# Attention readout with the values as the stationary operand, in two column halves, and denominators from the exponentials' running sums

## The chip, the cores and the metric

The program runs on one core of one Trainium2 chip. Times are device microseconds (us) of one execution; the figure that counts is the median of several. Engine names: PE is TensorE (PEld is its weight load), DVE is VectorE, ACT is ScalarE, POOL is GpSimd, SP is the engine that issues the weight DMAs.

## The reference, cut to what matters

Two layers over 256 tokens of width 1024. Layer 0 is a gated DeltaNet and is not touched. Layer 1 is a sparse attention with 16 query heads in 4 key/value groups, head width 64, and three branches: compressed keys (15 blocks), selected keys, and a window. With 256 tokens the selection takes every block and the window covers everything, so these two branches are plain causal attention with their own keys and values.

```
p_b   = softmax(mask(q @ k_b.T * scale))          for b in cmp, sel, win
o     = sum_b sigmoid(gate_b) * (p_b @ v_b) * silu(z_b)
out   = layer_norm(alpha * x + o @ w_out)
```

## The kernel before

Only the layer-1 attention and a copy ahead of it matter. PE, DVE, ACT and POOL each run their instructions in the order in which the program text emits them. The text emits work out of its natural order by two means: `defer(n, f)` holds `f` back until the n-th following `step()`, and `fills` is a list of projection units; `fill(n)` does n times "one step, then one unit". A unit (`tm_part`, L226) is six matmuls of 512 columns.

Queries are in two tiles of 128 tokens. Tile 0 is handled in units of two heads (it sees 128 keys), tile 1 in units of one head (256 keys), so that a unit always has four 128x128 blocks of probabilities. The 24 units come in a fixed order, one to a pass of the main loop (L1477), with numbers of fills at two places of each pass:

```
UNITS = "001010101101101101111111"
FA = "3113111011210212044211123"
FB = "0211121311122110212111000"
```

Pass i (0 to 24) does: `scores` of unit i on PE (L1318); `probs` of unit i-1 on ACT, which copies the transposed probabilities out of PSUM (L1367, L1371); a `step`; `maxima` of unit i on DVE (mask and row maxima, L1327 to L1334); FA[i] fills; a `merge` if one is due; `exps` of unit i on ACT (L1347 to L1352); the readout of the unit before; FB[i] fills; `transposes` of unit i on PE (L1360, L1362).

The readout before has the probabilities PT (128 keys x 128 queries) as the stationary operand and the values of a group, with a column of ones behind them, as 65 moving columns (L1386, L1389). Every such fp32 matmul is on record as two passes, each with its weight load. The ones column gives each softmax's denominator. The compressed branch of two heads is one matmul of 130 columns with 32 rows (L1392). The result of two heads (2 x 3 x 65 columns) lies in one PSUM bank, and `total` (L1398 to L1405), deferred by one step, does five DVE instructions on it: reciprocal of the denominators, times the gates, times the gated z, times the reciprocals, sum over the branches into zz. In tile 1 the two heads of a pair are read out one after the other, each in the pass after its own, where the units follow one another, else both at once.

PSUM has two banks of their own here, each with a single buffer:

```
def tbank(name):
    return pt_.tile([P, 512], F32, tag="t", name=name)
def obank(name):
    return pt_.tile([P, 512], F32, tag="o", name=name)
```

Before, `tbank` serves the transposes of the probabilities (L1357) and, late, those of `merge` (L1413), which turns zz back to features x tokens and splits it in a high part (ACT, L1422) and a low part (DVE, L1423); `obank` serves the readouts. Fills are the gate projection (bz, 48 units; its results go through ACT's tanh, L1218, and a DVE product, L1219, into zz) until pass 17, and the output projection (bo) from pass 19.

Ahead of the attention, `compress` (L1127) multiplies in two column halves: 61 stationary columns and 128 moving ones, the branches' results in partitions 0 to 60 and 64 to 124 (L1133). Its result is copied by ACT (L1139) and DVE (L1140), and `hidden` multiplies with it (L1148).

Of the kernel before, what the change touches and what calls it, by code (L numbers as in the profile page):

```python
# [93 lines left out]
def trunk(ctx: ExitStack, tc: tile.TileContext, I: dict, out: bass.AP):  # L94
# [925 lines left out]
    def rope(src, n, t, which, name, res):  # L1020
        co = cb[:, C_ROPE + (t * 4 + which) * 64:C_ROPE + (t * 4 + which + 1) * 64]
        si = cb[:, C_ROPE + (t * 4 + which + 1) * 64:C_ROPE + (t * 4 + which + 2) * 64]
        s3 = src.rearrange("p (a d) -> p a d", d=64)

        A = s3
        B = wk.tile([P, n, 64], F32, tag="ra", name=f"rb{name}", bufs=6)
# [12 lines left out]
        for q in range(n // 4):  # L1039
            res(q, lambda q=q: split(q))  # L1040
# [1 line left out]

    kh = wk.tile([P, 4, 528], F32R, name="kh", bufs=1)
    kl = wk.tile([P, 4, 528], F32R, name="kl", bufs=1)
    vt_ = wk.tile([P, 2, 2, 4, 65], F32, name="vtok", bufs=1)
    for a in range(2):
        for t in range(2):
            G.memset(vt_[:, a, t, :, 64:65], 1.0)
    kq = []

    def kv_done(c, t, ps):
        kind = c - 1
        S.copy(vt_[:, kind, t, :, 0:64], ps[:, 256:512].rearrange("p (a d) -> p a d", d=64))
# [38 lines left out]
    G.memset(hpS, 0.0)  # L1092
    hid = wk.tile([P, 2, 4, 16], F32, name="hid", bufs=1)
    G.memset(hid, 0.0)
    vbd = wk.tile([32, 4, 2, 65], F32, name="vbd", bufs=1)
    bd = cb[0:32, C_BD:C_BD + 2]
    G.tensor_copy(vbd[:, :, :, 64], bd[:, None, :].to_broadcast([32, 4, 2]))
    fill(2)
    k_post()
    fill(4)  # L1100
# [26 lines left out]
    def compress(n0):  # L1127
        w1 = [get(("w1", 2 * a + n0)).rearrange("p (m h) -> p m h", m=8) for a in range(2)]
        if n0 == 0:
            hps["t"] = obank("hpT")  # L1130
        for m in range(8):
            for a in range(2):
                PE.matmul(hps["t"][64 * a:64 * a + 61, 0:P], C2[n0][:, a, m, :], w1[a][:, m, :],  # L1133
                          start=n0 == 0 and m == 0, stop=n0 == 1 and m == 7)
        for a in range(2):
            used(("w1", 2 * a + n0))
        if n0:
            def copies():
                S.copy(hpS[0:61, :], hps["t"][0:61, 0:P])  # L1139
                V.tensor_copy(hpS[64:125, :], hps["t"][64:125, 0:P])  # L1140

            defer(1, copies)
# [34 lines left out]
    def compressed_v():  # L1177

        vcp = tbank("vcp")
        for g_ in range(4):  # L1180
            PE.matmul(vcp[0:32, g_ * 64:(g_ + 1) * 64], hr[:, g_].rearrange("p a b -> p (a b)"), w2[:, 256:320],
                      start=True, stop=True)

        def place():
            for g_ in range(4):
                V.tensor_tensor(vbd[:, g_, :, 0:64], vcp[0:32, None, g_ * 64:(g_ + 1) * 64].to_broadcast([32, 2, 64]),
                                bd[:, :, None].to_broadcast([32, 2, 64]), op=ALU.mult)

        defer(1, place)
# [22 lines left out]
    def bz_done(c, t, ps):  # L1212
        i = 2 * t + c // 3
        if i not in zz:
            zz[i] = wk.tile([P, 1536], F32, tag=f"zz{i}", name=f"zz{i}", bufs=1)
        zdone.add((c, t))
        th = wk.tile([P, 512], F32, tag="ra", name=f"th{c}{t}", bufs=6)
# [88 lines left out]
    S_, PT_, PTT, PC, PCT, MX, TP = {}, {}, {}, {}, {}, {}, {}  # L1306
    cnt = {"n": 0}

    def scores(u):
# [26 lines left out]
    def exps(u):  # L1336
# [6 lines left out]
        Pc = PC[t, h - h % 2]  # L1343
        if t == 0:
            for j in range(2):
                for b in range(2):
                    S.activation(pt[:, j, b, :], s4[:, j, b, :], AF.Exp, bias=mx[:, 2 * j + b:2 * j + b + 1])  # L1347
                S.activation(Pc[:, j, :], sp[:, j, 256:272], AF.Exp, bias=mx[:, 4 + j:5 + j])
        else:
            for b in range(2):  # L1350
                S.activation(pt[:, :, b, :], s4[:, :, b, :], AF.Exp, bias=mx[:, b:b + 1])  # L1351
            S.activation(Pc[:, h % 2, :], sp[:, 0, 256:272], AF.Exp, bias=mx[:, 4:5])  # L1352

    def transposes(u):
        t, h = u
# [19 lines left out]
    def readout(t, h, half=None):

        g_ = h // 4
        if half != 1:
            need_z(t, (h + 2) * 192)
            OP[t] = obank(f"op{t}{h}")  # L1380
        o3 = OP[t][:, 0:390].rearrange("p (r b d) -> p r b d", r=2, b=3)
        for r in range(2) if half is None else (half,):
            PT = PTT[0, h] if t == 0 else PTT[1, h + r]
            for b in range(2):
                if t == 0:
                    PE.matmul(o3[:, r, 1 + b, :], PT[:, r, b, :], vt_[:, b, 0, g_, :], start=True, stop=True)  # L1386
                else:
                    for j in range(2):
                        PE.matmul(o3[:, r, 1 + b, :], PT[:, j, b, :], vt_[:, b, j, g_, :], start=j == 0, stop=j == 1)  # L1389
        if half == 0:  # L1390
            return
        PE.matmul(o3[:, :, 0, :], PCT[t, h], vbd[:, g_, :, :], start=True, stop=True)  # L1392
        rc = sm.tile([P, 2, 3], F32, tag="rc", name=f"rc{t}{h}")
        o4 = o3[:, :, :, 0:64]

        o_ = zview(t, h * 192, 128).rearrange("p (r d) -> p r d", r=2)

        def total():  # L1398

            V.reciprocal(o3[:, :, :, 64], o3[:, :, :, 64])  # L1400
            V.tensor_tensor(rc, o3[:, :, :, 64], gt[:, t, h * 3:h * 3 + 6].rearrange("p (r b) -> p r b", b=3), op=ALU.mult)
            V.tensor_tensor(o4, o4, zview(t, h * 192, 384).rearrange("p (r b d) -> p r b d", r=2, b=3), op=ALU.mult)
            V.tensor_tensor(o4, o4, rc[:, :, :, None].to_broadcast([P, 2, 3, 64]), op=ALU.mult)
            V.tensor_reduce(o_, o4.rearrange("p r b d -> p r d b"), axis=AX.X, op=ALU.add)
# [64 lines left out]
    def merge1(g_):  # L1469
# [3 lines left out]
        if g_ == 3:  # L1473
            add_bo(1, [(1, g_)])

    n = len(units)
    for i in range(n + 1):  # L1477
        if i < n:
# [108 lines left out]
```

## Time and profile before

| | |
|---|---|
| median of 3 runs | 395.68 us (395.26 to 396.01) |
| profiled execution | 394.86 us, of which the span of the trace is 393.2 us |
| busy share of the span | PE 97%, PEld 85%, POOL 63%, DVE 57%, ACT 56% |
| granted PE clock | 0.996 of full, mean |
| attention's main loop | 241 to 372 us of the span |

The profile is one execution; its own time is 0.8 us under the median. A busy matmul lasts until its result has landed, so that neighbours overlap; what the engine spends on one is read from the distance between starts.

### The profile page before, as it was taken

How to read it: one execution, taken by the hardware profiler on the slowest of the kernel's cores; microseconds unless marked ns; L12 is line 12 of the kernel's file. 1: busy time of each engine (PE TensorE's matmuls, PEld its weight loads, DVE VectorE, ACT ScalarE, POOL GpSimd, SP SyncE). 2: the span in 40 equal slices, each digit the busy share in tenths (PEclk: the TensorE clock that was granted, in tenths of full speed). 3: DMA queues.
4: the chain of work that ended last, by engine and by line, in shares of the span. 5: the costliest groups of instructions: out<-in, count | busy, mean ns of one | idle time of the engine just before them, and what ended most of it. 6: DMA issues, size and time to landing. Idle time of an engine off the chain costs nothing.

```text
span 393.2 us, 7550 instructions
## 1 busy us (share of the span) xinstructions
PE 380.0 (97%) x2870; PEld 335.4 (85%) x2870; DVE 223.0 (57%) x590; ACT 220.8 (56%) x434; POOL 246.2 (63%) x154
## 2 busy tenths in 40 slices
PE   7999999999999999999999999999999999999991
PEld 6999999999989987877998788888888888778891
DVE  2868776668533455454541655545655555676726
ACT  5788666655654372615563649566465657456410
POOL 5699999747454856894755978184554728109051
PEclk9999999999999999999999999999999999999998
DMA  6966579745334314563536863242515333301011
GB/s 225 331 223 233 191 236 283 196 123 163 110 109 156 113 52 163 181 248 110 209 108 213 304 233 122 93 163 107 162 53 161 99 117 113 103 3 53 3 53 53
DMA packets 23476, 58.68 MB, mean 149 GB/s; under 512 B 6672, under 2 KB 9232, under 8 KB 23312
## 3 DMA queue, kind: packets, MB, share of 16 engines
q1 hardware_dynamic: 23232, 58.13, 44.0%
q8 instruction: 22, 0.36, 0.4%
q14 instruction: 14, 0.11, 0.1%
q10 hardware_dynamic: 144, 0.07, 0.1%
q0 software_dynamic: 64, 0.01, 0.0%
HBM read 55.96 MB, written 2.23 MB: 148 GB/s over the span
## 4 chain that ended last, share of the span: by engine, by line
PE 48%; DVE 3%; POOL 1%; DMA 1%; ACT 1%; issue 0%; POOLq 0%; DVEq 0%; SPq 0%; ACTq 0%
PE pbz L233 6%; PE pbz L234 5%; PE pbz L235 5%; PE op L1389 4%; PE s L1318 3%; PE ptp L1360 2%; PE pbq L233 2%; PE op L1392 2%; PE pbq L235 2%; PE pbq L234 2%; PE op L1386 1%; POOL lo_skv L185 1%; DMA raw_bq<-in_bq 1%; PE pskv L235 1%; PE pbo L233 1%; PE pskv L233 1%
## 5 line engine op out<-in xcount | busy, mean ns | idle before, releaser
L185 POOL TENSOR_TENSOR lo_bz<-raw_bz,hi_bz 128x1024 fp32r<-128x1024 f32 x24 | 56.8, 2387 | 39.7 <-ACT hi_bz L181 22.1
L185 POOL TENSOR_TENSOR lo_wqkv<-raw_wqkv,hi_wqkv 128x1024 fp32r<-128x1024 f32 x22 | 52.6, 2409 | 6.7 <-ACT hi_wqkv L181 4.5
L233 PE MATMUL pbz<-hi_bz,x1h 128*128 128x512 f32 x96 | 38.9, 405 | 0.0
L234 PE MATMUL pbz<-hi_bz,x1l 128*128 128x512 f32 x96 | 37.7, 393 | 0.0
L235 PE MATMUL pbz<-lo_bz,x1h 128*128 128x512 f32 x96 | 37.6, 392 | 0.0
L185 POOL TENSOR_TENSOR lo_bo<-raw_bo,hi_bo 128x1024 fp32r<-128x1024 f32 x8 | 18.9, 2386 | 23.9 <-ACT hi_bo L181 18.7
L185 POOL TENSOR_TENSOR lo_skv<-raw_skv,hi_skv 128x1024 fp32r<-128x1024 f32 x12 | 28.4, 2394 | 5.0 <-PE pskv L235 5.0
L185 POOL TENSOR_TENSOR lo_wz<-raw_wz,hi_wz 128x1024 fp32r<-128x1024 f32 x8 | 19.4, 2441 | 16.9 <-ACT hi_wz L181 16.9
L1367 ACT COPY PT<-ptp 128x512 f32<-128x512 f32 x24 | 14.1, 588 | 24.4 <-PE ptp L1360 24.4
L181 ACT CAST hi_bz<-raw_bz 128x1024 fp32r<-128x1024 f32 x24 | 25.3, 1052 | 2.8 <-DMA raw_bz<-in_bz 1.6
L185 POOL TENSOR_TENSOR lo_wo<-raw_wo,hi_wo 128x1024 fp32r<-128x1024 f32 x8 | 19.0, 2387 | 11.5 <-ACT hi_wo L181 11.5
L185 POOL TENSOR_TENSOR lo_bq<-raw_bq,hi_bq 128x1024 fp32r<-128x1024 f32 x8 | 19.1, 2392 | 10.9 <-ACT hi_bq L181 6.4
L181 ACT CAST hi_wqkv<-raw_wqkv 128x1024 fp32r<-128x1024 f32 x22 | 22.7, 1042 | 0.8 <-DMA raw_wqkv<-in_wqkv 0.8
L235 PEld LDWEIGHTS pbz<-lo_bz,x1h 128*128 128x128 f32 x96 | 18.0, 188 | 4.1
L233 PEld LDWEIGHTS pbz<-hi_bz,x1h 128*128 128x128 f32 x96 | 18.0, 188 | 4.1
L234 PEld LDWEIGHTS pbz<-hi_bz,x1l 128*128 128x128 f32 x96 | 18.0, 188 | 2.8
L1351 ACT ACTIVATE pt<-s,mx 128x256 f32<-128x256 f32 x32 | 13.4, 471 | 10.9 <-DVE mx L1334 8.7
L215 PE MATMUL pk<-xh,hi_wqkv 128*128 128x256 f32 x64 | 18.7, 292 | 0.0
L215 PE MATMUL pq<-xh,hi_wqkv 128*128 128x256 f32 x64 | 18.5, 289 | 0.0
L217 PE MATMUL pk<-xh,lo_wqkv 128*128 128x256 f32 x64 | 18.1, 283 | 0.0
L217 PE MATMUL pq<-xh,lo_wqkv 128*128 128x256 f32 x64 | 18.1, 283 | 0.0
L216 PE MATMUL pk<-xl,hi_wqkv 128*128 128x256 f32 x64 | 18.1, 283 | 0.0
(360 smaller groups left out, 1255.9 us busy)
## 6 DMA issues: line engine op xcount, KB each, us to landing
raw_bz<-in_bz SPq DMA_DIRECT2D x24, 512.0 KB, 3.4
raw_wqkv<-in_wqkv SPq DMA_DIRECT2D x23, 512.0 KB, 4.4
raw_skv<-in_skv SPq DMA_DIRECT2D x12, 512.0 KB, 3.2
raw_wz<-in_wz SPq DMA_DIRECT2D x8, 512.0 KB, 3.6
raw_wo<-in_wo SPq DMA_DIRECT2D x8, 512.0 KB, 3.3
raw_bq<-in_bq SPq DMA_DIRECT2D x8, 512.0 KB, 3.4
raw_bo<-in_bo SPq DMA_DIRECT2D x8, 512.0 KB, 3.3
raw_w<-in_w SPq DMA_DIRECT2D x4, 512.0 KB, 3.2
```

Source lines behind the costliest of these rows:

```text
L181: S.copy(h, r)
L185: e.tensor_tensor(l, r, h.bitcast(F32), op=ALU.subtract)
L215: PE.matmul(ps[:, 0:T], wh[:, kt, :], ah[:, kt, :], start=kt == 0, stop=False)
L216: PE.matmul(ps[:, 0:T], wh[:, kt, :], al_[:, kt, :], start=False, stop=False)
L217: PE.matmul(ps[:, 0:T], wl[:, kt, :], ah[:, kt, :], start=False, stop=kt == 7)
L233: PE.matmul(ps, ah[:, kt, tt], wh[:, k4, cols], start=kt == 0, stop=False)
L234: PE.matmul(ps, al_[:, kt, tt], wh[:, k4, cols], start=False, stop=False)
L235: PE.matmul(ps, ah[:, kt, tt], wl[:, k4, cols], start=False, stop=kt == 7)
L1318: PE.matmul(sp[:, j, 0:n], lq, kk[:, hh // 4, c0:c0 + n], start=i == 0, stop=i == 1)
L1351: S.activation(pt[:, :, b, :], s4[:, :, b, :], AF.Exp, bias=mx[:, b:b + 1])
L1367: S.copy(PT.rearrange("p a b c -> p (a b c)"), TP[u])
L1389: PE.matmul(o3[:, r, 1 + b, :], PT[:, j, b, :], vt_[:, b, j, g_, :], start=j == 0, stop=j == 1)
```

## The change

The two large branches' readout swaps its operands: the values (128 keys x 64) become stationary, the probabilities PT the 128 moving columns, and the branches write the two halves of the partitions (0 to 63, 64 to 127) of `tbank`. DVE copies the result to SBUF (oS), and a new step, `turn_back`, transposes it per head into `obank`, where the compressed branch's matmul and `total` follow. `turn_back` is called where `turn()` stands: after the fills of FA and of FB if there are any, ahead of a further readout, and in a merge that waits. Tile 1 is read out a pair of heads at a time. The ones columns go; each exponential instead gives the sum of its row as a second output (`accum_out`), and `total` takes the reciprocal of these sums. The tag "ra" (PT, tanh, rope) has 5 buffers for 6, PcT 3 for 2. The copy L1139 moves from ACT to DVE.

```diff
-    vt_ = wk.tile([P, 2, 2, 4, 65], F32, name="vtok", bufs=1)
-            G.memset(vt_[:, a, t, :, 64:65], 1.0)
+    vt_ = wk.tile([P, 2, 2, 4, 64], F32, name="vtok", bufs=1)
...
-                S.copy(hpS[0:61, :], hps["t"][0:61, 0:P])
+                V.tensor_copy(hpS[0:61, :], hps["t"][0:61, 0:P])
                 V.tensor_copy(hpS[64:125, :], hps["t"][64:125, 0:P])
...
-                    S.activation(pt[:, j, b, :], s4[:, j, b, :], AF.Exp, bias=mx[:, 2 * j + b:2 * j + b + 1])
-                S.activation(Pc[:, j, :], sp[:, j, 256:272], AF.Exp, bias=mx[:, 4 + j:5 + j])
+                    S.activation(pt[:, j, b, :], s4[:, j, b, :], AF.Exp, bias=mx[:, 2 * j + b:2 * j + b + 1],
+                                 accum_out=den[:, j, 1 + b:2 + b])
+                S.activation(Pc[:, j, :], sp[:, j, 256:272], AF.Exp, bias=mx[:, 4 + j:5 + j], accum_out=den[:, j, 0:1])
...
-    def readout(t, h, half=None):
+    def readout(t, h):
         g_ = h // 4
-        if half != 1:
-            need_z(t, (h + 2) * 192)
-            OP[t] = obank(f"op{t}{h}")
-        o3 = OP[t][:, 0:390].rearrange("p (r b d) -> p r b d", r=2, b=3)
-        for r in range(2) if half is None else (half,):
+        tb = tbank(f"ot{t}{h}")
+        for r in range(2):
             PT = PTT[0, h] if t == 0 else PTT[1, h + r]
-            for b in range(2):
-                if t == 0:
-                    PE.matmul(o3[:, r, 1 + b, :], PT[:, r, b, :], vt_[:, b, 0, g_, :], start=True, stop=True)
-                else:
-                    for j in range(2):
-                        PE.matmul(o3[:, r, 1 + b, :], PT[:, j, b, :], vt_[:, b, j, g_, :], start=j == 0, stop=j == 1)
+            for j in range(1 + t):
+                for b in range(2):
+                    PE.matmul(tb[64 * b:64 * b + 64, r * P:(r + 1) * P], vt_[:, b, j, g_, :], PT[:, j if t else r, b, :],
+                              start=j == 0, stop=j == t)
+        oS = wk.tile([P, 2, P], F32, tag="oS", name=f"oS{t}{h}", bufs=2)
+        V.tensor_copy(oS.rearrange("p a b -> p (a b)"), tb[:, 0:2 * P])
+        backs.append(lambda: turn_back(t, h, oS))
+
+    def turn_back(t, h, oS):
+        need_z(t, (h + 2) * 192)
+        op = obank(f"op{t}{h}")
+        o3 = op[:, 0:384].rearrange("p (r b d) -> p r b d", r=2, b=3)
+        for r in range(2):
+            PE.transpose(op[:, r * 192 + 64:r * 192 + 192], oS[:, r, :], ident)
+        PE.matmul(o3[:, :, 0, :], PCT[t, h], vbd[:, h // 4, :, :], start=True, stop=True)
...
-            V.reciprocal(o3[:, :, :, 64], o3[:, :, :, 64])
+            V.reciprocal(rd, DEN[t, h])
...
+    def turn():
+        while backs:
+            backs.pop(0)()
...
         fill(int(FA[i]))
+        if int(FA[i]):
+            turn()
...
             if t == 0:
+                turn()
                 readout(t, h)
...
-                if (units[i - 2] if h % 2 else units[i]) == (1, h ^ 1):
-                    readout(t, h - h % 2, h % 2)
-                elif h % 2:
+                if h % 2:
+                    turn()
                     readout(t, h - 1)
...
         fill(int(FB[i]))
+        if int(FB[i]):
+            turn()
         if i < n:
             transposes(units[i])
     while len(merges) > 1:
         advance()
         fill(1)
+    turn()
```

## Rows read from the trace of the kernel before

**Rows 1.** Waits of PE from 318 us on: us in total, times, longest.

```profile
PE op L1389 <- DVE zz L1404: 0.6, 2, 0.4
```

**Rows 2.** PE's timeline around a tile-0 readout: start us, length, instruction.

```profile
254.86 1.00 PE L1386 MATMUL op<-vtok,PT 128*128 128x65 f32 x8
...
256.55 0.39 PE L234 MATMUL pbz<-hi_bz,x1l 128*128 128x512 f32 x1
256.78 0.39 PE L235 MATMUL pbz<-lo_bz,x1h 128*128 128x512 f32 x1
```

**Rows 3.** PE's timeline, a tile-1 readout of a pair, pass 15.

```profile
332.04 1.89 PE L1389 MATMUL op<-vtok,PT 128*128 128x65 f32 x16
333.86 0.48 PE L1392 MATMUL op<-vbd,PcT 32*128 32x130 f32 x2
334.28 0.66 PE L1360 MATMUL ptp<-ident,pt 128*128 128x128 f32 x4
334.69 0.37 PE L1318 MATMUL s<-kh,qT 128*128 128x272 f32 x1
```

**Rows 4.** PE's timeline around `compress`, two column halves; last row: the line's durations.

```profile
207.90 0.39 PE L235 MATMUL pbq<-lo_bq,x1h 128*128 128x512 f32 x1
208.22 1.97 PE L1133 MATMUL hpT<-raw_w,C 128*61 128x128 f32 x32
210.12 0.50 PE L233 MATMUL pbq<-hi_bq,x1h 128*128 128x512 f32 x1
210.45 0.39 PE L234 MATMUL pbq<-hi_bq,x1l 128*128 128x512 f32 x1
...
L1133 PE MATMUL hpT<-raw_w,C x64: 272/273/321, 208.2 to 214.8; 128*61 128x128 f32 x64
```

**Rows 5.** Timeline of pass 13 (tile 0): last scores, ACT's exponentials, transposes.

```profile
318.71 0.29 PE L1318 MATMUL s<-kl,qT 128*128 128x272 f32 x1
...
321.22 0.28 ACT L1348 ACTIVATE Pc<-s,mx 128x16 f32<-128x16 f32 x1
321.38 0.64 ACT L1347 ACTIVATE pt<-s,mx 128x128 f32<-128x128 f32 x2
321.88 0.30 ACT L1348 ACTIVATE Pc<-s,mx 128x16 f32<-128x16 f32 x1
...
322.97 0.60 PE L1360 MATMUL ptp<-ident,pt 128*128 128x128 f32 x4
```

**Rows 6.** Timeline of pass 16: a total in front of the maxima on DVE.

```profile
335.15 0.29 PE L1318 MATMUL s<-kl,qT 128*128 128x272 f32 x1
...
334.38 0.20 DVE L1400 RECIPROCAL op<-op 128x6 f32<-128x6 f32 x1 [2.19 <-PE op L1392]
...
336.50 0.72 DVE L1327 TENSOR_TENSOR s<-s,cb 128x544 f32<-128x544 f32 x1
```

**Rows 7.** Timeline of pass 9: a gate product in front of the maxima.

```profile
294.77 0.28 PE L1318 MATMUL s<-kl,qT 128*128 128x256 f32 x1
...
296.36 0.42 DVE L1331 TENSOR_TENSOR s<-s,cb 128x256 f32<-128x256 f32 x1
```

**Rows 8.** Timeline of pass 18 (tile 1), with a merge.

```profile
344.14 0.28 PE L1318 MATMUL s<-kl,qT 128*128 128x256 f32 x1
...
345.27 0.42 DVE L1331 TENSOR_TENSOR s<-s,cb 128x256 f32<-128x256 f32 x1
...
346.63 0.68 DVE L1423 TENSOR_TENSOR x1l<-tp_b,x1h 128x512 fp32r<-128x512 f32 x1
...
347.54 0.28 ACT L1352 ACTIVATE Pc<-s,mx 128x16 f32<-128x16 f32 x1
...
347.75 0.44 PE L1360 MATMUL ptp<-ident,pt 128*128 128x128 f32 x2
```

**Rows 9.** DVE's groups by line and form: a copy of 256 PSUM columns.

```profile
L1275 DVE COPY gf<-gp 96x256 f32<-96x256 f32 x1 | 0.4, 409 | 0.0
```

**Rows 10.** Waits of PE from 200 to 241 us.

```profile
PE hp L1148 <- DVE hpS L1140: 0.6, 1, 0.6
```

More of the change, by code (lines that the diff above doesn't have):

```diff
@@ L1025, in rope @@
         A = s3
-        B = wk.tile([P, n, 64], F32, tag="ra", name=f"rb{name}", bufs=6)
+        B = wk.tile([P, n, 64], F32, tag="ra", name=f"rb{name}", bufs=5)
         V.tensor_tensor(B[:, :, 0:32], s3[:, :, 32:64], si[:, None, 0:32].to_broadcast([P, n, 32]), op=ALU.mult)
@@ L1044, in trunk @@
     kl = wk.tile([P, 4, 528], F32R, name="kl", bufs=1)
-    vt_ = wk.tile([P, 2, 2, 4, 65], F32, name="vtok", bufs=1)
-    for a in range(2):
-        for t in range(2):
-            G.memset(vt_[:, a, t, :, 64:65], 1.0)
+    vt_ = wk.tile([P, 2, 2, 4, 64], F32, name="vtok", bufs=1)
     kq = []
@@ L1052, in kv_done @@
         kind = c - 1
-        S.copy(vt_[:, kind, t, :, 0:64], ps[:, 256:512].rearrange("p (a d) -> p a d", d=64))
+        S.copy(vt_[:, kind, t, :, :], ps[:, 256:512].rearrange("p (a d) -> p a d", d=64))
         rope(ps[:, 0:256], 4, t, 2, f"k{kind}{t}",
@@ L1094, in trunk @@
     G.memset(hid, 0.0)
-    vbd = wk.tile([32, 4, 2, 65], F32, name="vbd", bufs=1)
+    vbd = wk.tile([32, 4, 2, 64], F32, name="vbd", bufs=1)
     bd = cb[0:32, C_BD:C_BD + 2]
-    G.tensor_copy(vbd[:, :, :, 64], bd[:, None, :].to_broadcast([32, 4, 2]))
     fill(2)
@@ L1185, in place @@
             for g_ in range(4):
-                V.tensor_tensor(vbd[:, g_, :, 0:64], vcp[0:32, None, g_ * 64:(g_ + 1) * 64].to_broadcast([32, 2, 64]),
+                V.tensor_tensor(vbd[:, g_, :, :], vcp[0:32, None, g_ * 64:(g_ + 1) * 64].to_broadcast([32, 2, 64]),
                                 bd[:, :, None].to_broadcast([32, 2, 64]), op=ALU.mult)
@@ L1216, in bz_done @@
         zdone.add((c, t))
-        th = wk.tile([P, 512], F32, tag="ra", name=f"th{c}{t}", bufs=6)
+        th = wk.tile([P, 512], F32, tag="ra", name=f"th{c}{t}", bufs=5)
         S.activation(th, ps, AF.Tanh, scale=0.5)
@@ L1305, in trunk @@
     units = [order0.pop(0) if k == "0" else order1.pop(0) for k in UNITS]
-    S_, PT_, PTT, PC, PCT, MX, TP = {}, {}, {}, {}, {}, {}, {}
+    S_, PT_, PTT, PC, PCT, MX, TP, DEN = {}, {}, {}, {}, {}, {}, {}, {}
     cnt = {"n": 0}
@@ L1342, in exps @@
             PC[t, h] = wk.tile([P, 2, 16], F32, tag="Pc", name=f"Pc{t}{h}", bufs=4)
-        Pc = PC[t, h - h % 2]
+            DEN[t, h] = sm.tile([P, 2, 3], F32, tag="den", name=f"den{t}{h}", bufs=6)
+        Pc, den = PC[t, h - h % 2], DEN[t, h - h % 2]
         if t == 0:
@@ L1346, in exps @@
                 for b in range(2):
-                    S.activation(pt[:, j, b, :], s4[:, j, b, :], AF.Exp, bias=mx[:, 2 * j + b:2 * j + b + 1])
-                S.activation(Pc[:, j, :], sp[:, j, 256:272], AF.Exp, bias=mx[:, 4 + j:5 + j])
+                    S.activation(pt[:, j, b, :], s4[:, j, b, :], AF.Exp, bias=mx[:, 2 * j + b:2 * j + b + 1],
+                                 accum_out=den[:, j, 1 + b:2 + b])
+                S.activation(Pc[:, j, :], sp[:, j, 256:272], AF.Exp, bias=mx[:, 4 + j:5 + j], accum_out=den[:, j, 0:1])
         else:
             for b in range(2):
-                S.activation(pt[:, :, b, :], s4[:, :, b, :], AF.Exp, bias=mx[:, b:b + 1])
-            S.activation(Pc[:, h % 2, :], sp[:, 0, 256:272], AF.Exp, bias=mx[:, 4:5])
+                S.activation(pt[:, :, b, :], s4[:, :, b, :], AF.Exp, bias=mx[:, b:b + 1],
+                             accum_out=den[:, h % 2, 1 + b:2 + b])
+            S.activation(Pc[:, h % 2, :], sp[:, 0, 256:272], AF.Exp, bias=mx[:, 4:5], accum_out=den[:, h % 2, 0:1])
     def transposes(u):
@@ L1365, in probs @@
         t, h = u
-        PT = PTT[u] = wk.tile([P, 2, 2, P], F32, tag="ra", name=f"PT{t}{h}", bufs=6)
+        PT = PTT[u] = wk.tile([P, 2, 2, P], F32, tag="ra", name=f"PT{t}{h}", bufs=5)
         S.copy(PT.rearrange("p a b c -> p (a b c)"), TP[u])
@@ L1369, in probs @@
             h -= h % 2 * t
-            PCT[t, h] = wk.tile([32, P], F32, tag="PcT", name=f"PcT{t}{h}", bufs=2)
+            PCT[t, h] = wk.tile([32, P], F32, tag="PcT", name=f"PcT{t}{h}", bufs=3)
             S.copy(PCT[t, h], S_[u][0:32, 1, 272:400])
-    OP, summed = {}, set()
-    def readout(t, h, half=None):
+    summed = set()
+    backs = []
+    def readout(t, h):
         g_ = h // 4
-        if half != 1:
-            need_z(t, (h + 2) * 192)
-            OP[t] = obank(f"op{t}{h}")
-        o3 = OP[t][:, 0:390].rearrange("p (r b d) -> p r b d", r=2, b=3)
-        for r in range(2) if half is None else (half,):
-            PT = PTT[0, h] if t == 0 else PTT[1, h + r]
-            for b in range(2):
-                if t == 0:
-                    PE.matmul(o3[:, r, 1 + b, :], PT[:, r, b, :], vt_[:, b, 0, g_, :], start=True, stop=True)
-                else:
-                    for j in range(2):
-                        PE.matmul(o3[:, r, 1 + b, :], PT[:, j, b, :], vt_[:, b, j, g_, :], start=j == 0, stop=j == 1)
-        if half == 0:
-            return
-        PE.matmul(o3[:, :, 0, :], PCT[t, h], vbd[:, g_, :, :], start=True, stop=True)
+        tb = tbank(f"ot{t}{h}")
+        for r in range(2):
+            PT = PTT[0, h] if t == 0 else PTT[1, h + r]
+            for j in range(1 + t):
[5 more added lines that the diff above has]
+        backs.append(lambda: turn_back(t, h, oS))
@@ L1393, in readout @@
+    def turn_back(t, h, oS):
[5 more added lines that the diff above has]
+        PE.matmul(o3[:, :, 0, :], PCT[t, h], vbd[:, h // 4, :, :], start=True, stop=True)
         rc = sm.tile([P, 2, 3], F32, tag="rc", name=f"rc{t}{h}")
-        o4 = o3[:, :, :, 0:64]
         o_ = zview(t, h * 192, 128).rearrange("p (r d) -> p r d", r=2)
+        rd = op[:, 384:390].rearrange("p (r b) -> p r b", r=2)
@@ L1398, in total @@
         def total():
-            V.reciprocal(o3[:, :, :, 64], o3[:, :, :, 64])
[L1401 to L1404, printed above, removed]
+            V.reciprocal(rd, DEN[t, h])
@@ L1405, in total @@
+            V.tensor_tensor(rc, rd, gt[:, t, h * 3:h * 3 + 6].rearrange("p (r b) -> p r b", b=3), op=ALU.mult)
+            V.tensor_tensor(o3, o3, zview(t, h * 192, 384).rearrange("p (r b d) -> p r b d", r=2, b=3), op=ALU.mult)
+            V.tensor_tensor(o3, o3, rc[:, :, :, None].to_broadcast([P, 2, 3, 64]), op=ALU.mult)
+            V.tensor_reduce(o_, o3.rearrange("p r b d -> p r d b"), axis=AX.X, op=ALU.add)
             summed.add((t, h))
@@ L1510, in trunk @@
         fill(1)
+    turn()
     add_bo(1, [(1, g_) for g_ in range(3)])
```

## Prediction

> **What bounds the kernel now.** I read PE's waits first, then PE's timeline, then the same passes on DVE and ACT. From 318 us to the end PE's longest waits by name, for the bank of the readouts, come to 0.6 us [rows 1]: in the attention PE issues nearly without a gap, so whatever PE no longer does is saved, and whatever new wait stands ahead of one of its instructions is lost. The second reading decides the sum: how near each pass is to such a wait. Call S the end of a unit's last scores and T the start of its transposes. Between them PE has fills and a readout; in the same time DVE does the maxima and ACT the exponentials, which the transposes read. In pass 13, with three fills, S is 319.00, T 322.97, and the exponentials end at 322.18 [rows 5]: a margin of 0.79 us for a chain of 3.18 us. Each addition to that chain beyond the margin stops PE.
>
> **PE's own work.** An ordinary 512-column matmul takes 0.23 us (256.55 to 256.78); the tile-0 readout block, with the compressed branch, takes 256.55 - 254.86 - 0.23 = 1.46 us [rows 2]. A tile-1 pair takes 334.28 - 332.04 = 2.24 us [rows 3], and 0.1 for the next full-width matmul's late start, as below: 2.35. The new readout has a model in the trace: `compress` also has some 64 stationary columns, 128 moving ones and two halves in turn. Its 32 passes of 0.27 us fill 1.97 us, so one follows another every (1.97 - 0.27)/31 = 0.055 us; the whole block takes 210.45 - 207.90 - 2x0.23 = 2.09 us, of which 0.34 is at its edges [rows 4] (210.12 to 210.45 is 0.1 over the ordinary 0.23). So a tile-0 readout takes 8x0.055 + 0.34 = 0.78 us and a tile-1 pair 16x0.055 + 0.34 = 1.22. Turning back adds two transposes at 0.41/4 each, the compressed branch's 0.42 [rows 3] and 0.1 at either edge: 0.83. Tile 0: 0.78 + 0.83 - 1.46 = +0.15, eight times +1.2 us; tile 1: 1.22 + 0.83 - 2.35 = -0.30, eight times -2.4. The readout is halved, but PE keeps only 1.2 us of it.
>
> The copy L1139 goes to DVE: PE waits 0.6 us for L1140 [rows 10], which waits for ACT, busy with a weight cast. Both copies on an idle DVE are done under the fill: -0.7 us, if nothing after it is late (nothing else is waited for there). The ones columns were written off the path: nothing. Five "ra" buffers: in the order of the new text each PT is read out before five later allocations, so nothing waits; if it did, ACT's tanh would.
>
> **What enters the chains.** Four things.
>
> The sums. No exponential in the trace has a second output. From below it costs nothing, from above as much as a small instruction of its own, 0.28 us (the compressed branch's). I take the distance such an instruction adds, 321.22 to 321.38 = 0.16 [rows 5], since a sum of one column is most like it: six a tile-0 unit, 0.96 us; three a tile-1 unit, 0.48.
>
> `total` before the maxima. Before, a fill stands behind most readouts and carries `total`, which DVE does before the scores. Now `turn_back` comes after the last fill, so the next step is the one between scores and maxima, and `total` stands in DVE's queue ahead of them. Pass 16 has this order already, for want of a fill: S is 335.44, the total runs from 334.38, the maxima start at 336.50, 1.06 late, a total taking 2.12 [rows 6]. From the loop's order this now happens in passes 2, 3, 5, 6, 7, 9, 10, 12, 13, 15, 17, 18, 19 and 21. A gate product carried by that step does the same; pass 9 shows it, 1.31 late [rows 7], and it moves to passes 6, 11, 14 and 16.
>
> The bank. Readouts move to `tbank`, which has one buffer and holds the transposes. So the next transposes wait for the copy to SBUF: 0.41 for 256 columns [rows 9], 0.65 with the way there and back (estimate; the copy can be 0.3 to 0.7 with latencies). Queued behind PE's waiting transposes are the next scores and everything else. A fill covers it; where FB is 0 nothing does. In passes 18, 20 and 22 a merge takes the bank first, and the readout then waits for the merge's subtraction, which stands behind the maxima on DVE. The Trainium skill (TensorEngine Tiling, section PSUM Bottleneck) warns that tiling speeds up TensorE but not the evacuation; by it the gain above is not to be counted at all, which would leave the sum 1.2 us higher.
>
> Now each pass, chain against cover. A fill is 6x0.2275 = 1.365; cover is PE's work less 0.13 (the scores' tail: 3.97 in pass 13). The chains' needs: tile 0, 3.18 less 0.6, since four transposes are issued over 0.41 and the last exponential is wanted behind them (estimate): 2.58. Tile 1 from pass 18 [rows 8]: S 344.42, exponentials' end 347.82, the maxima 0.85 late, hence 3.40 - 0.81 = 2.59, less 0.3: 2.3. A total ahead adds 1.06 - 0.04, a gate product 1.31 - 0.04.
> - Passes 7, 10, 13 (tile 0, three fills, total ahead): 2.58 + 1.02 + 0.96 = 4.56 against 3.97: 0.6 each, 1.8.
> - Pass 6 (gate product and whole total ahead): 2.3 + 1.27 + 2.12 + 0.48 = 6.17 against 2.73 + 0.78 + 0.83 - 0.13 = 4.21: 1.9.
> - Pass 16 (tile 0, gate product): 4.81 against 2.73 + 0.83 - 0.13 = 3.43: 1.4.
> - Passes 19 and 21 (tile 1, total): 3.8 against one fill and four transposes, 1.68, and two fills and two transposes, 2.8: 2.1 and 1.0.
> - The bank: passes 15 and 24, a copy uncovered, 0.65 each; pass 17, where the last gate product is in the copy's way too, 1.1; pass 18, the subtraction ends 2.89 after S [rows 8], now 3.1, PE having 0.3 of work: 2.8, and a copy: 3.45; pass 20, 1.0 (two transposes, ACT's cast, the subtraction); pass 22, 1.0 and a copy: 1.65.
> - The rest (2, 3, 5, 9, 11, 12, 14 and those without anything ahead) have cover enough, some by less than 0.3.
>
> Sum 16.7 us. PE already loses some in passes 16, 18 and 19: pass 18 has 3.33 from S to T for 0.41 + 2.24 - 0.13 = 2.5 of work [rows 3, 8], 0.8; three such are 2.4. So +14.3 - 1.2 - 0.7 = +12.4: 394.86 + 12.4 = 407.3 for the profiled execution, which lies 0.8 under the median: **408.1 us**. Bounds: sums that cost nothing take off 0.96 or 0.48 wherever a chain with them sets the stall, 5 us in all (403); at 0.28 they add 4 (412).
>
> **Rivals.**
> - *The bank alone.* The sums are free and the transposes, which need only part of the exponentials, slip past the rest. Left are passes 15, 17, 18, 20, 22, 24: 8.5 - 0.8 for what pass 18 loses already - 1.9 = +5.8, 401.5 us. For it: most margins are missed by under 1 us. Against: pass 6 and 16 miss by far more.
> - *Faster: PE alone sets the time.* Then -1.2 - 0.7: 393.8 us. It decides if DVE and ACT are ready before PE in every pass, which takes a margin of 0.79 us to hold 1.02 + 0.96 less 0.6. The waits of before speak for it: so few [rows 1]. Against it the late maxima of passes 9 and 16 are there to be read. The Trainium skill's swap recipe (TensorEngine Tiling, When to Use Tiling: values as stationary, 2x column tiling) is this rival; the trace's 0.055 against 0.11 agrees for the readout by itself.
> - *The halves don't run together* in this readout: 0.055 more for each of 8x8 + 8x16 = 192 passes, +10.5: 418.6. `compress` has the same shapes, so little speaks for it.
> - *Gains and losses cancel*, between the first two: 395 to 399.
>
> **How the numbers follow.** The forecast has 0.55 (own range 403 to 413), the bank alone 0.20, faster 0.13, cancelling 0.07, no overlap 0.05. The predicted time is 408.0. The range, 397 to 414, takes in the forecast with its bounds, the bank alone and the upper part of cancelling; left out are the faster rival, the one of no overlap and the tails. Faster by over 0.2% (about what a measurement of this kernel can tell) 0.13; within 0.2% 0.05, from cancelling; slower 0.82.
>
> **What would show it.** Right: 16 readouts whose passes start 0.055 us apart, and PE's total time for readouts, turning back and compressed branches some 1 us lower; PE waiting for ACT's exponentials at the transposes of passes 6, 7, 10, 13, 16, 19, 21, and for DVE's merge product or the copy at the readouts or transposes of passes 15, 17, 18, 20, 22; maxima starting about 1 us after the scores in the passes named; an ACT sweep of tile 0 near 2.4 us for 1.47; no wait at L1148. Wrong, if the maxima still start 0.04 after S, if a sum leaves the exponentials' spacing as it was, or if PE's waits by name stay under 2 us.

## The result

The changed kernel takes 411.1 us (median of 4 runs, 410.43 to 411.94) against 395.77 us before (395.26 to 396.01): 15.3 us more, a ratio of 1.0388 with a 95% interval of 1.0356 to 1.0419. The forecast was 408.0 with a range of 397 to 414. Slower, by about as much as forecast; but some 4 of the 15.3 us came from a step that the forecast had put at nothing, and the sums were priced too high.

The page of the changed kernel begins with the span, each engine's busy time with its share, and, in 40 slices, PE's granted clock:

```profile
span 410.1 us, 7717 instructions
PE 385.0 (94%) x2902; PEld 328.9 (80%) x2902; DVE 227.9 (56%) x607; ACT 229.7 (56%) x529; POOL 246.2 (60%) x149
PEclk9999999999999999989999999999999999969998
```

PE's share falls from 97 to 94% of a longer span: PE now waits. And the clock, full before except in the last slice, dips in two slices well inside the kernel. PE's waits by name, over the whole span (total us, times, longest):

```profile
PE ot L1384 <- DVE x1l L1427: 4.1, 3, 2.3
PE op L1395 <- DVE oS L1387: 3.9, 4, 1.7
PE ktp L1058 <- DVE x1l L962: 2.2, 1, 2.2
PE ptp L1359 <- DVE oS L1387: 1.2, 2, 0.6
...
PE qtp L1201 <- DVE kl L1168: 0.7, 1, 0.7
...
PE ptp L1359 <- ACT pt L1344: 0.3, 1, 0.3
...
PE ptp L1359 <- ACT pt L1349: 0.2, 1, 0.2
```

From 318 us on, before had three short lines in this view, 1.2 us in all; [rows 1] shows the largest. Now the readout (L1384) waits for the merge's subtraction (L1427), the turning back (L1395) and the transposes (L1359) for the copy to SBUF (L1387). These are the bank's waits of the forecast. The third line, ktp, lies at 181 us, long before the attention: nobody had asked for it. The wait at the product with `hpS` [rows 10] is gone, as forecast; part of it is given back later at qtp.

Where the 16.9 us of span came from, by how much later the same PE instruction starts: 0.5 at the first loads, 3.85 between 165 and 190 us, -0.7 at `hidden`, 0.9 at qtp, 11.4 in the main loop, 1.1 behind it. By pass, from the first scores of one to those of the next (the forecast is its stall, less 0.8 in 16, 18 and 19 for what before loses there, and +0.15 or -0.30 for a readout; passes between which work moves stand together):

| passes | change, us | forecast |
|---|---|---|
| 1, 2, 8, 11, 14 (tile-0 readout, covered) | +0.09 to +0.13 each | +0.15 |
| 5, 9, 12 (tile-1 pair, covered) | -0.37, -0.36, -0.18 | -0.30 |
| 6 (gate product and total ahead) | +2.01 | +2.05 |
| 7, 10, 13 (total ahead) | +0.41, +0.65, +0.45 | +0.6 |
| 0 | +0.36 | 0 |
| 15 and 16 (a turn back now falls in 16) | +0.32 | +0.95 |
| 4 and 17 (a fill of 4 now falls in 17) | +1.32 | +1.4 |
| 18 | +2.80 | +2.35 |
| 19, 20, 21, 22 together (+0.60, +1.54, -0.09, +1.43) | +3.47 | +3.5 |
| 3 | 0.00 | 0 |

Passes 19 to 22 have to be taken together. Before, the pairs of passes 20 and 22 were read out half in the pass ahead (eight of the sixteen passes stand in 19 and in 21, some 0.9 us each by [rows 3]); now both halves stand in 20 and 22, and the turning back of the second falls in 23. Their stalls in the forecast are 1.3, 1.0, 1.0 and 1.65 us; with two readouts at -0.30 and 0.83 moved out, that is +3.5.

The loop's sum is +11.4; with what follows it 12.5, for a forecast of 13.1. The span grew by 16.9 us and the median by 15.3, mainly because the profiled execution of the changed kernel lies 0.84 us above its median and that of before 0.9 under.

Pass 6 shows the order of DVE's queue. The timeline of the changed kernel (start us, length, instruction; in brackets idle before and what ended it):

```profile
282.66 0.28 PE L1314 MATMUL s<-kl,qT 128*128 128x256 f32 x1
...
283.64 0.69 DVE L1215 SCALAR_TENSOR_TENSOR zz<-th,pbz 128x512 f32<-128x512 f32 x1 [5.00 <-ACT th L1214]
...
283.94 0.39 PE L235 MATMUL pbz<-lo_bz,x1h 128*128 128x512 f32 x1
284.24 0.19 DVE L1403 RECIPROCAL op<-den 128x6 f32<-128x6 f32 x1
284.26 0.66 PE L1384 MATMUL ot<-PT,vtok 128*64 128x128 f32 x8
...
285.18 0.40 PE L234 MATMUL pbz<-hi_bz,x1l 128*128 128x512 f32 x1
...
286.34 0.42 DVE L1327 TENSOR_TENSOR s<-s,cb 128x256 f32<-128x256 f32 x1
...
287.71 0.41 DVE L1387 COPY oS<-ot 128x256 f32<-128x256 f32 x1
...
288.18 0.44 PE L1395 MATMUL op<-ident,oS 128*128 128x128 f32 x2 [1.68 <-DVE oS L1387]
```

The last scores start at 282.66; the maxima wait behind a gate product and a whole `total` until 286.34, 3.68 later (3.40 after those scores have ended). The copy stands behind the maxima, and PE, out of fills, waits 1.68 us for it. The same rows give the readout's price: 285.18 - 283.94 - 2x0.23 = 0.78 us, the forecast's figure to the hundredth.

Pass 18 shows the bank, and what follows from a long wait:

```profile
356.37 0.68 DVE L1427 TENSOR_TENSOR x1l<-tp_b,x1h 128x512 fp32r<-128x512 f32 x1
...
357.10 1.09 PE L1384 MATMUL ot<-PT,vtok 128*64 128x128 f32 x16 [2.27 <-DVE x1l L1427]
...
358.25 0.42 DVE L1387 COPY oS<-ot 128x256 f32<-128x256 f32 x1 [1.20 <-PE ot L1384]
...
358.73 0.44 PE L1395 MATMUL op<-ident,oS 128*128 128x128 f32 x2 [0.53 <-DVE oS L1387]
359.09 0.79 PE L1396 MATMUL op<-vbd,PcT 32*128 32x128 f32 x2
359.82 1.11 PE L1359 MATMUL ptp<-ident,pt 128*128 128x128 f32 x4
```

The merge holds the bank until DVE has subtracted, which stands behind total and maxima (the same pass before is in [rows 8]); the readout loses 2.27 us, its copy another 0.53. The last two lines compare with [rows 3]: four transposes 1.11 us instead of 0.66, the compressed branch 0.79 instead of 0.48. PE's clock had fallen; the table by stretch (length; busy time of PE, PEld, DVE, ACT, POOL; granted clock; DMA) says so:

```profile
181.10:184.90 3.80, 3.75 (x12) 3.08 (x13) 3.05 (x8) 1.72 (x5) 0.00 (x0) 0.56 0.03 10
...
350.00:359.00 9.00, 4.91 (x45) 3.42 (x43) 5.40 (x13) 4.36 (x16) 0.10 (x1) 1.00 0.19 60
359.00:366.00 7.00, 7.00 (x28) 5.83 (x26) 4.00 (x10) 3.38 (x9) 0.14 (x1) 0.51 0.00 0
366.00:380.00 14.00, 12.71 (x79) 9.80 (x77) 8.60 (x22) 8.10 (x22) 9.34 (x4) 1.00 0.10 37
```

Behind the waits of pass 18 PE, though busy throughout, runs for some 7 us at 0.51 of the full clock, the lower of its two levels (1.2 GHz), and behind the wait at ktp for 3.8 us at 0.56 (mean of the stretch). Pass 19 lies wholly in the first of these stretches.

The sums are instructions of their own. The first exponentials of pass 0, on ACT:

```profile
248.93 0.37 ACT L1344 ACTIVATE pt<-s,mx 128x128 f32<-128x128 f32 x1
249.18 0.21 ACT L1344 ACTIVATION_READ_ACCUMULATOR pt<-s,mx 128x1 f32 x1
249.28 0.38 ACT L1344 ACTIVATE pt<-s,mx 128x128 f32<-128x128 f32 x1
249.53 0.22 ACT L1344 ACTIVATION_READ_ACCUMULATOR pt<-s,mx 128x1 f32 x1
249.62 0.29 ACT L1346 ACTIVATE Pc<-s,mx 128x16 f32<-128x16 f32 x1
```

Two exponentials are 0.35 us apart. But the reads overlap their neighbours: a sweep of tile 0, to the end of its last exponential, takes 1.93 us for 1.47 (+0.46 for six sums), one of tile 1 1.19 for 1.00 (+0.19 for three), 0.06 to 0.08 us a sum. The forecast had 0.16.

### The profile page after: what moved, and what is told of

The parts are those of the page before. It is cut to its first block, busy times and chain, and to the rows that moved or that the text cites. A ratio compares the mean times of both kernels' runs of the same rounds, so it can differ in the third digit from the quotient of the medians.

```text
span 410.1 us, 7717 instructions
## 1 busy us (share of the span) xinstructions
PE 385.0 (94%) x2902; PEld 328.9 (80%) x2902; DVE 227.9 (56%) x607; ACT 229.7 (56%) x529; POOL 246.2 (60%) x149
## 4 chain that ended last, share of the span: by engine, by line
PE 42%; DVE 8%; ACT 3%; DMA 3%; issue 1%; POOL 1%; POOLq 0%; SPq 0%; DVEq 0%; ACTq 0%
PE pbz L233 5%; PE pbz L234 4%; PE pbz L235 4%; PE ptp L1359 3%; PE ot L1384 3%; PE s L1314 2%; DMA raw_bz<-in_bz 2%; PE op L1396 1%; PE pbq L233 1%; PE pbq L235 1%; PE pbq L234 1%; DMA cb<-in_cb 1%; PE pskv L233 1%; PE pskv L234 1%; PE pskv L235 1%
## 5 line engine op out<-in xcount | busy, mean ns | idle before, releaser
L185 POOL TENSOR_TENSOR lo_bq<-raw_bq,hi_bq 128x1024 fp32r<-128x1024 f32 x8 | 19.1, 2400 | 12.5 <-ACT hi_bq L181 8.0
L185 POOL TENSOR_TENSOR lo_wo<-raw_wo,hi_wo 128x1024 fp32r<-128x1024 f32 x8 | 19.0, 2387 | 11.4 <-ACT hi_wo L181 11.4
L1215 DVE SCALAR_TENSOR_TENSOR zz<-th,pbz 128x512 f32<-128x512 f32 x12 | 8.2, 687 | 24.4 <-ACT th L1214 24.4
L1349 ACT ACTIVATE pt<-s,mx 128x256 f32<-128x256 f32 x32 | 14.9, 471 | 12.2 <-DVE mx L1330 12.2
L1359 PE MATMUL ptp<-ident,pt 128*128 128x128 f32 x96 | 18.3, 300 | 2.2 <-DVE oS L1387 1.2
L1344 ACT ACTIVATE pt<-s,mx 128x128 f32<-128x128 f32 x32 | 11.5, 371 | 12.2 <-DVE mx L1325 12.2
```

The costliest lines, as they stand in the source:

```text
L185: e.tensor_tensor(l, r, h.bitcast(F32), op=ALU.subtract)
L1359: PE.transpose(tp[:, (2 * j + b) * P:(2 * j + b + 1) * P], pt[:, j, b, :], ident)
```

## The experiments

### Where the 3.85 us ahead of the attention come from

The wait at ktp ends a chain that begins in SP's queue. Changed kernel, timeline of SP's queue, DVE and PE:

```profile
158.90 14.46 SPq L161 DMA_DIRECT2D raw_skv<-in_skv  x6
173.45 0.38 SPq L1007 DMA_DIRECT2D cb<-in_cb  x1
...
178.06 0.29 DVE L1027 TENSOR_TENSOR rbk<-pskv,cb 128x128 f32<-128x128 f32 x1 [7.99 <-DMA cb<-in_cb]
...
181.16 0.77 PE L1058 MATMUL ktp<-ident,hlk 128*128 128x128 f32 x4 [2.22 <-DVE x1l L962]
181.57 0.78 PE L233 MATMUL pskv<-hi_skv,x1h 128*128 128x512 f32 x1
182.15 0.63 PE L234 MATMUL pskv<-hi_skv,x1l 128*128 128x512 f32 x1
```

The kernel before, the same queue:

```profile
158.14 7.41 SPq L161 DMA_DIRECT2D raw_skv<-in_skv  x4
165.64 0.38 SPq L1007 DMA_DIRECT2D cb<-in_cb  x1
```

From 155 us on, the load of the constants cb stands behind six weight loads, where before it stood behind four; its first reader on DVE waits 8 us, and PE 2.22 for what is behind that reader. The next ktp follows 7.58 us later (181.16 to 188.74) instead of 5.92: 1.66 more at the lower clock (the 512-column matmuls 0.43 apart for 0.23). Together that is 3.88 us, the shift of 3.85.

Nothing in the change touches this load. Of its edits I suspected the four one-element-wide memsets of the ones columns on POOL, which the change removes. Two kernels test it from both sides: the changed kernel with four such memsets on an unused tile, and the kernel before with its four written later.

```diff
+    dm = wk.tile([P, 2, 2, 4, 1], F32, name="dm", bufs=1)
+    for a in range(2):
+        for t in range(2):
+            G.memset(dm[:, a, t, :, :], 1.0)
```

> The changed kernel with the four small POOL memsets of the ones columns put back, on a tile that nothing reads. Theory (queue): their removal let the program's build put the load of the constants two weight loads later in SP's queue, so that the rotation ahead of the attention waited for it (3.9 us); with them back the constants load as before and the time is 411.1 - 3.9 = 407.2 us, or 406.3 if the late weights behind it cost 0.9 more. Rival (chance): the 3.9 us is jitter of the weight DMAs; then 411 us.

> The kernel before with the same four memsets emitted later, beside that of hid. Queue theory: the constants load late here too, 395.8 + 3.9 = 399.7 us. Rival (jitter, or the changed kernel's SBUF layout): 395.8 us.

The changed kernel with the memsets: 406.6 us (406.24 to 406.9; ratio 1.0285, 1.0270 to 1.0301), 4.5 less, or 4.1 by the two ratios, each to runs of before beside it. Its load of cb in SP's queue, behind four weight loads again:

```profile
158.25 7.42 SPq L161 DMA_DIRECT2D raw_skv<-in_skv  x4
165.76 0.38 SPq L1007 DMA_DIRECT2D cb<-in_cb  x1
```

The kernel before with late memsets: 399.02 us (ratio 1.0087, 1.0062 to 1.0111, that is 3.4 us more). Its load of cb is issued at 173.43 us, behind six weight loads, and the wait of the changed kernel is in its list of PE's waits:

```profile
PE ktp L1058 <- DVE x1l L962: 2.3, 1, 2.3
```

So the memsets' place decides, with no attention edit involved. They take 0.10 us each, and in the changed kernel with them they run at 167.6 us, behind the issue of cb at 165.76: it is not their running that lets the load go early. What their place sets is the order in which the loads come to stand in SP's queue. By which rule the order comes out so stays open: only the two orders were seen.

### The copy L1139 alone

The kernel before with only the `hpS` copy moved to DVE.

```diff
-                S.copy(hpS[0:61, :], hps["t"][0:61, 0:P])
+                V.tensor_copy(hpS[0:61, :], hps["t"][0:61, 0:P])
```

> The kernel before with the first half of the hpS copy on DVE as in the change, nothing else. If the wait of 0.7 us ahead of hidden's matmul is saved for good: 395.1 us. Rival: it is given back at the next late weight or cast: 395.8 us.

394.81 us, ratio 0.9983 (0.9969 to 0.9996). Run once more beside the one-pair kernel below:

> The kernel before with the hpS copy on DVE, on the same chip as the run with one pair, to have both against the same runs of before. Theory: 394.8 us, 0.4 to 0.7 under before. Rival, that the gain of the first run was chance: no difference.

394.49 us (12 runs), ratio 0.9964 (0.9949 to 0.9979). Of PE's waits between 200 and 241 us none is left in the first of these two runs (before, [rows 10]); in the second one of 0.4 us stands at qtp. This edit gains 0.2 to 0.4%.

### The sums

The changed kernel with the memsets, and exponentials without their second output. The denominators are left out: `total` divides by ones.

```diff
...
-                S.activation(pt[:, :, b, :], s4[:, :, b, :], AF.Exp, bias=mx[:, b:b + 1],
-                             accum_out=den[:, h % 2, 1 + b:2 + b])
+                S.activation(pt[:, :, b, :], s4[:, :, b, :], AF.Exp, bias=mx[:, b:b + 1])
...
```

> As a1_memsets, but the exponentials give no sums: total takes the reciprocal of a tile of ones, so the denominators are left out. Theory (the sums lengthen a chain that is already too long): the tile-0 sweep goes from 1.93 back to 1.47 us and the tile-1 sweep from 1.19 to 1.00; passes 0, 7, 10, 13 and 16, which the sweep's end sets, lose 0.36 to 0.46 us each and pass 6 0.19: 2.2 us off, 404.4 us. Rival (the sums are hidden behind the vector queue and the bank): under 0.5 us off, 406.2 or more. The price forecast for a sum, 0.16 us, would give 4 us off, 402.6.

405.21 us (404.37 to 405.92; ratio 1.0242, 1.0205 to 1.0278), 1.4 under the kernel with sums; the intervals of the two ratios just meet. Pass by pass it is plainer: 0, 7, 10, 13 and 16 become shorter by 0.36, 0.42, 0.63, 0.40 and 0.55, together 2.4 us, and the stalls of 0, 7, 10 and 13 are gone entirely: these passes are as long as before. Pass 6 keeps its 7.16 us where 0.19 less was expected, so its stall is not the exponentials'. Pass 19 gains 0.77, but pass 18 loses 0.87, for a reason that has nothing to do with sums: the fall of the clock comes earlier here and catches the readout itself. From the table by stretch:

```profile
349.80:356.50 6.70, 6.17 (x33) 5.07 (x34) 3.00 (x8) 1.02 (x3) 0.00 (x0) 0.50 0.00 0
```

and from the timeline, sixteen passes of the readout in 1.98 us that take 1.09 at full clock:

```profile
349.80 1.98 PE L1388 MATMUL ot<-PT,vtok 128*64 128x128 f32 x16 [2.27 <-DVE x1l L1431]
```

### Turning back earlier

The changed kernel with the memsets; `turn` comes behind the first fill of FB, so that another fill (where there are two) stands behind it and carries `total`.

```diff
-        fill(int(FB[i]))
-        if int(FB[i]):
+        k = int(FB[i])
+        fill(min(k, 1))
+        if k:
             turn()
+        fill(max(k - 1, 0))
```

> As a1_memsets, but where FB has two or three fills the turn back stands after the first of them, so that the next fill's step carries total and it no longer stands ahead of the next maxima. Theory (vector queue): pass 6 falls from 7.16 to some 5.4 us, pass 13 from 5.58 to some 5.2; the passes after FB = 1 stay as they are: 2.1 us off, 404.5 us. Rival (total is late wherever it stands, since it only moves the copy or the gate product behind it): under 0.5 us off.

405.05 us (404.74 to 405.5; ratio 1.0233, 1.0203 to 1.0262), 1.55 less. Pass 6 falls from 7.16 to 5.29 us, pass 13 from 5.58 to 5.14, and no other changes by more than 0.1. Where FB of the pass ahead is 2, the total no longer stands in front: the maxima of pass 6 start 1.31 us late instead of 3.40, those of 13 0.24 for 1.08; those of 2 and 12 are as early again (0.13 and 0.04), but there was no stall to cure.

### The bank

The changed kernel with the memsets, where readout and turning back share one tile of `obank`: the copy to SBUF stays, but `tbank` is left to the transposes and merges.

```diff
-        tb = tbank(f"ot{t}{h}")
+        tb = obank(f"ot{t}{h}")
...
-    def turn_back(t, h, oS):
+    def turn_back(t, h, oS, op):
...
-        op = obank(f"op{t}{h}")
```

> As a1_memsets, but the readout goes into the bank of its own (o) and is turned back in place there, once DVE has copied it out, so that neither the transposes of the probabilities nor a merge share a bank with a readout. Theory (bank): passes 15, 18, 20 and 22 lose 0.6, 1.2, 0.9 and 1.5 us of their waits, 4.2 in all: 403 us beside 407.2 for a1. Rival (the vector queue and the sums set these passes): under 1.5 us less than a1.

404.07 us (402.5 to 408.37; ratio 1.0239, 1.0179 to 1.0298), 2.5 less where the theory had 4.2; the interval overlaps that of the kernel with the memsets (1.0270 to 1.0301), so the total alone does not show a gain. By pass in the profiled execution it is plainer: passes 15, 18, 20 and 22 fall by 0.66, 2.21, 1.02 and 1.33, 5.2 together. But passes 6 and 12 rise by 1.94 and 1.03, with a wait that the theory had not got:

```profile
PE ot L1388 <- DVE zz L1410: 3.8, 3, 2.3
```

The readout now waits for the `total` before it, which holds `obank`: 2.25 us in pass 6, where it was 1.68 for the copy, and 1.20 in pass 12, for 0.14. The rest of pass 6's rise, 1.4 us, goes with the clock, which falls behind this wait. The table by stretch, columns as above:

```profile
282.90:286.30 3.40, 3.40 (x12) 2.37 (x11) 0.71 (x4) 1.28 (x6) 0.00 (x0) 0.50 0.46 161
```

Both banks are bad where the other user is late: `tbank` where a merge or nothing but transposes follows, `obank` where the total before is not done. So the next kernel takes `tbank` early and `obank` from pass 15 on, and turns back behind the first fill:

```diff
-        tb = tbank(f"ot{t}{h}")
+        own = h == 14 or (t == 1 and h >= 6)
+        tb = (obank if own else tbank)(f"ot{t}{h}")
```

> e6, and from pass 15 on the readout in place in the bank o as in e4, not before it. Theory (bank from pass 15 on, total's place before): the 5.2 us that e4 took off passes 15, 18, 20 and 22 without the 2.9 it lost in passes 6 and 12: 404.5 - 5.2 = 399.3 us. Rival: the total of one pair now holds the bank of the next readout in the late passes too: 401 us or more.

399.6 us (398.87 to 400.12; ratio 1.0093, 1.0062 to 1.0123), 5.45 under the one with the turning back alone. By pass, 15, 18, 20 and 22 fall by 0.66, 2.20, 0.96 and 1.36. Part of the 2.20 is the clock: with the turning back alone it stands at 0.50 for the last 2.3 us of pass 18, here at 1.00 throughout, which is up to 1.2 us (an estimate, half of the 2.3). The x1l wait is gone; what is left of PE's longest:

```profile
PE ot L1401 <- DVE oS L1392: 2.9, 3, 1.2
```

### The new readout where it is covered

The kernel before with the `hpS` copy on DVE, and the new readout for the tile-1 pairs of heads 0 and 1 and of heads 4 and 5 only (sums for these heads alone; ones columns, and so the memsets, kept).

```diff
+        if t == 1 and h in NEW:
+            if half != 0:
+                readout_new(h)
+            return
```

> The kernel before with the hpS copy on DVE (b1), and the new readout for two pairs of tile 1 alone, heads 0 and 4, whose passes 5 and 12 have two fills behind the readout: turned back after the first, total carried by the second, sums for these four heads only. If PE's price is right (a pair 0.30 us cheaper) and nothing waits: 394.8 - 0.6 = 394.2 us, 0.997 of the kernel before. Rival: the copy or the sums take it back: 394.8 us or more.

395.52 us (ratio 0.999, 0.9974 to 1.0006): no gain over the copy alone. Pass 5, which reads the first pair, is 0.31 us shorter (7.56 to 7.25), the forecast's -0.30. Pass 12, which reads the second, is 0.50 longer. Its timeline:

```profile
312.36 0.59 ACT L1374 COPY PT<-ptp 128x512 f32<-128x512 f32 x1 [1.01 <-PE ptp L1367]
...
312.99 0.85 PEld L1389 LDWEIGHTS ot<-PT,vtok 128*64 128x64 f32 x16 [0.34 <-ACT PT L1374]
...
315.58 0.41 DVE L1392 COPY oS<-ot 128x256 f32<-128x256 f32 x1
...
316.05 0.44 PE L1401 MATMUL op<-ident,oS 128*128 128x128 f32 x2 [0.38 <-DVE oS L1392]
```

FA is 0 there. No fill stands between the transposes and the readout, which waits 0.34 us until ACT has emptied their bank, and the copy stands behind a gate product and the maxima, 0.38. That is 0.72 against a gain of 0.30, which makes 0.42 of the 0.50. With the first pair alone:

> The kernel before with the hpS copy on DVE and the new readout for one tile-1 pair only (heads 0 and 1, read out in pass 5 with a fill before and two behind). In the run with two pairs pass 5 was 0.31 us shorter than in the kernel with the hpS copy alone, as the price of a covered pair says (-0.30), and pass 12, where no fill stands ahead of the readout, 0.50 longer. Theory that the price holds wherever a fill stands before and behind: 394.5 us, 0.3 under the hpS copy alone, pass 5 at 7.25. Rival, that the pair's gain is given back later in the loop: 394.8 to 395.2.

394.37 us (12 runs), ratio 0.9962 (0.9946 to 0.9979), beside 394.49 for the copy alone. Pass 5 again takes 7.25 us for 7.56, but a gain of 0.3 can't be told apart in the totals. It and the copy alone are the only versions that beat the kernel before; of the readout's change, nothing measurable is in that.

## Why the prediction was right, and where it was not

**PE alone.** Right in the covered passes: +0.09 to +0.13 for +0.15; -0.18 to -0.37 for -0.30, and -0.31 in the kernels with one and two new pairs. The readout by itself takes the forecast's 0.78 us, its passes 0.055 apart, so the halves do run together; turning back eats the gain. The faster rival, and the one of no overlap, fall here.

**"The ones columns were written off the path: nothing."** This step failed. The instructions cost nothing, but their absence put the load of cb behind two more weight loads, and that cost 3.4 us (put into the kernel before) to 4.5 us (taken out of the changed one). The forecast looked for who waits for the memsets, and not for what their removal reorders.

**hpS, -0.7.** The wait went as forecast, and alone the edit is worth 0.7 and 1.4 us by its two ratios. In the full change 0.9 came back at qtp; that wait is gone with the memsets, there again (0.7) with one and with two new pairs, and there (0.4) in one of the two runs of the copy alone, and what sets it was not tried.

**Sums, 0.16 each.** Mis-sized: 0.06 to 0.08. The sum's place was right: where a total is ahead too, the sums decide (7, 10 and 13 stall with them, not without). That these three came out near the forecast's 0.6 is luck: by its own sum, with 0.46 us of sums for 0.96, they would stall 2.58 + 1.02 + 0.46 - 3.97 = 0.09 us, and they lost 0.41 to 0.65. So the 0.6 us taken off the chain for transposes that start ahead of the last exponential was too much as well; 0.2 to 0.3 fits passes 0, 7, 10 and 13 (an estimate from their lengths and the starts of their maxima). The two errors cancel. The lower bound, 5 us off if sums cost nothing, is reached only if 0.96 goes from stalls put at 0.6; by pass, 2.4 us went. Pass 0 was missed: already before, its exponentials end 4.08 us after the scores and its transposes start at 3.97, so it had no margin at all, and the forecast's list leaves it out.

**Total and gate product ahead of the maxima.** Right: 0.95 to 1.07 late in passes 2, 3, 5, 7, 9, 12, 15, 18 and 21 (1.06 forecast), 1.33 and 1.14 in 10 and 13, 3.40 in pass 6 (1.31 + 2.12 forecast), and the order alone is worth 2.3 us in passes 6 and 13. The rival of the bank alone (401.5) falls with these passes and with 7 and 10, where PE stalls and no readout waits for the bank. Two passes have the right size for another reason. In pass 6 (+2.01 for +2.05) the forecast had the transposes wait for the exponentials; PE waits at the turning back instead, for the copy behind the maxima, and without sums the pass is no shorter. In pass 19 the maxima start only 0.22 late (and 0.04 in 17), because PE itself had waited in the pass before and the total was done meanwhile. Pass 19 has no wait of PE of 0.1 us or more; it runs at 0.51 of the clock instead. In the kernel with the readouts in `obank` pass 18 waits less, and there pass 19 is as forecast: granted clock 1.00, maxima 1.08 late, and a wait of 1.0 us for the exponentials at the transposes.

**The bank.** Right, and the largest part: keeping the readouts out of `tbank` from pass 15 on gives 5.45 us (up to 1.2 of it by the clock in pass 18), and the copy in pass 15 costs 0.66 (forecast 0.65). The warning of the Trainium skill (TensorEngine Tiling, PSUM Bottleneck) that tiling does not speed up the evacuation holds: here PE waits 5.1 us for copies of 0.42 us (the lines of L1395 and L1359 with oS above), in 6 of the 16 readouts, more than the 1.2 us of PE's own work that the change takes off in the forecast.

**The clock** had no term. Behind each of the two long waits PE ran at about half rate; 1.66 us of the ktp stretch are read as that. The Trainium skill (TensorE: Matmul & The Clock Gate, Part 1) says that a gate sets the rate by how busy PE has been, and halves it after idling; the traces agree, with granted clocks of 0.56 and 0.51 behind the two long waits. The wait of 1.68 us in pass 6 of the changed kernel was followed by no fall (granted clock 1.00 from 240 to 350 us), that of 2.25 us in the kernel with the readouts in `obank` was. The clock's share in passes 18 and 19 can't be split off, since DVE's chain sets their end in part.

So the total was 3.0 us short by the medians. The sum belongs to the profiled execution, and there it was 4.6 short (407.3 for 411.94): 0.5 at the first loads, 3.85 around ktp and 0.9 at qtp had no term, and the loop with what follows came out 0.6 lower than forecast. The other 1.6 us are luck: the profiled execution lies 0.84 above its median, where the forecast took 0.8 under.

Of the 15.3 us, the memsets take 4.5, the place of the turning back 1.55, the late bank 5.45 (by the ratios 4.1, 2.1 and 5.5); of the 3.8 left, some 2 are the sums in passes 0, 7, 10 and 16, and the rest, not taken apart by a run, goes with the waits that remain in 17 and 18 (1.16 and 1.65 us) and the stalls of 19 and 21, less what the copy and the covered pairs save.

## What to carry to other kernels

A shorter operation on the busiest engine is worth its own saving only where the step that it adds on another engine is covered; price the added copy pass by pass, with what stands ahead of it in that engine's queue and what else the bank serves. When an instruction is removed, look also at what the program order of the loads makes of it: compare the order of the DMA queue before and after, even in stages that the change does not touch. When stalls follow one another, ask of the second what caught up during the first: queued work gets done while the engine waits. And compare passes over a stretch that holds all of their work: half a readout that moves to the next pass looks like a gain in one and a stall in the other.

## What was not expected of the hardware

- An exponential with a sum issues a second ACT instruction of some 0.2 us (ACTIVATION_READ_ACCUMULATOR), but in a row of exponentials it adds only 0.06 to 0.08 us each.
- A wait of PE of 2.22 us, among shorter ones, was followed by 3.8 us at 0.56 of the clock, and the waits of pass 18 (2.27 and 0.53 us) by 7 us at 0.51, while PE had work throughout. Without sums the same pass fell before its readout, which then took 1.98 us for 1.09.
- Four memsets of 0.10 us on POOL decide whether a load is issued at 165.7 or 173.5 us on another engine's queue.
